# A decoder layer with 32 experts: the first norm's factor and shift moved behind the gather, routing reordered, the last expert weights in halves

## The chip, the cores and the metric

The kernel runs on one core of one Trainium2 chip. The metric is the device time of one execution in microseconds (us). The kernel before takes 873.96 us, the median of three runs (873.03, 873.96 and 874.01).

## What is computed

One layer of a decoder on 512 tokens of width 1024, in float32. A projection feeds a pooling mixer and a stick-breaking attention; their gated sum is projected out. Then come the first norm, a mixture of 32 experts in 4 groups, a gated embedding, and the second norm:

```
x = LayerNorm(alpha * x + merged @ w_o)                 (y * g + b, with ln1_g and ln1_b)
x = LayerNorm(alpha * x + HMoE(x) + sigmoid(x @ w_pg) * (p[i] @ w_pp))
...
g_idx = jnp.argmax(group_probs, axis=-1)
...
top_vals, top_idx = lax.top_k(sel_logits, TOP_K_IN_GROUP)
top_w = jax.nn.softmax(top_vals, axis=-1) * g_prob[:, None]
...
        h = jax.nn.silu(xt @ w_eg[g, e]) * (xt @ w_eu[g, e])
        y = y + (h @ w_ed[g, e]) * combine[:, g, e, None]
```

Each token goes to the two best experts of its best group. The expert weights are the bulk of what is read: 32 experts of 6 MB.

## The kernel before, in words

**Tiles and stages.** Tokens are in four blocks of 128 (tb 0 to 3). Products in float32 that need accuracy are made from a high and a low part (`mm3`, lines 143 to 145). After attention, `out_proj` multiplies the merged rows by w_o; `residual` adds alpha times x and takes statistics, `moments` and `shift` make factor and shift of a row, and `normalise` (ScalarE, L767) applies them. `gain` (L770) multiplies by the row g1 and `offset` (L773) adds the row b1, on VectorE or GpSimd; `affine` is both. `keep_high` (ScalarE, L786) and `keep_low` (L789) keep the result, called x1, as a high and a low part of 128x1024 per block, with its columns in another order.

**Routing.** `turn` transposes a block on TensorE (copies L595 on ScalarE, differences L596 on VectorE); `route` makes logits from the turned rows, which are not yet multiplied by g: the router's weights carry g and b. `fold_logits` (L617) adds the parts up. `choose` (L634 to L653, VectorE, for two blocks) finds group and experts and ends in the mask msk. `place` (L659 to L663) counts positions on TensorE; `count_tokens` (L670 on) and `rank` (L686 on) order the experts by their number of tokens. `order` holds their numbers, and the loads of all but three experts take the number from it.

**Experts.** Experts run in 12 units of 2, 3 or 4 (KINDS "pm" "pp" "qqq" "pppp" "m"; p is two, m three, q four). A unit has 128 slots for tokens, and `gather` (L848) fills them: x1's parts are multiplied by a one-hot matrix G, and `keep_slots` (L865, ScalarE, and L867, VectorE) copies a bank of PSUM into xg. `inner` (L907) makes two products with the weights eg and eu, `outer` (L1115) one with ed. `pair` runs a unit j: inner, outer, the gathers for the next two units, and the scatter of the unit before (`scatter_steps`). In unit 0, `renew` (L899) adds x1's parts up again for all four blocks in acc, and ScalarE multiplies them by alpha (L1085).

**Loads.** The weights are 192 chunks of 1 MB (`elist`). The tuple FIRST names 18 that are loaded ahead, with the pool that each lies in ("s8" is a pool of 8 tiles of 8 KB per partition, "wraw", "whi", "wlo", "acc" and "more" are others). From then on a chunk is loaded when a tile comes free: `eload_past` after a product in `inner` or `outer`, in the order `sequence`. SyncE issues all loads (L536, the halves L541) in this order. The last two chunks of the last unit are loaded in column halves. In units 3 to 6 the embedding runs between the products (`embedding`), with `split_transpose` turning x1.

**End.** In the last unit `split_acc` splits the accumulators; then, per block, a sum is opened with a product of the identity and these parts (L1290), the last unit's scatter is added (L1293), and statistics and the second norm follow.

Inside `with tc.manual_schedule()` each engine's instructions run in the order in which the program writes them.

Of the kernel before, what the change touches and what calls it, by code (L numbers as in the profile page):

```python
# [37 lines left out]
def layer_kernel(ctx: ExitStack, tc: tile.TileContext, x, p, w_in, w_pool, pool_scale, w_pu, w_au,  # L38
# [730 lines left out]
    def gain(tb, h, eng):  # L769
        eng.tensor_mul(acc[tb][:, halves[h]], acc[tb][:, halves[h]], g1[:, halves[h]])  # L770

    def offset(tb, h, eng):
        eng.tensor_add(acc[tb][:, halves[h]], acc[tb][:, halves[h]], b1[:, halves[h]])  # L773

    def affine(tb, h, eng):
        gain(tb, h, eng)
        offset(tb, h, eng)

# [607 lines left out]
```

## Time and profile before

| what | value |
| --- | --- |
| median of three runs | 873.96 us |
| the profiled execution | 873.73 us |
| span in its trace | 871.9 us |
| TensorE busy | 805.8 us (92%) |
| VectorE busy | 412.3 us (47%) |
| ScalarE busy | 214.2 us (25%) |
| GpSimd busy | 191.4 us (22%) |
| DMA | 241.89 MB, 276 GB/s read and written over the span |

PE is TensorE's products, PEld its weight loads, DVE VectorE, ACT ScalarE, POOL GpSimd, SP SyncE; SPq is SyncE's issuing of transfers. The times in a row count from the start of the span. A row of a timeline can stand for several equal instructions in a row (x4). Brackets at a row's end give the idle time of the engine before it, and what released it. PEclk is the clock that TensorE was granted, 1.00 being 2.4 GHz and 0.50 being 1.2 GHz. Busy shares are means over stages with different limits.

### The profile page before, as it was taken

What the parts mean: (1) busy time and instruction counts of PE and PEld (TensorE: products, weight loads), DVE (VectorE), ACT (ScalarE), POOL (GpSimd) and SP (SyncE); (2) the same over time, 40 slices, a digit from 0 to 9 for tenths busy, and PEclk for the clock granted to TensorE, in tenths of its full rate; (3) what the DMA queues carried; (4) which work ended last, traced back from release to release, by engine and by line L of the source; (5) the groups of instructions that cost most, each with busy time, mean ns of one, the idle gap of its engine ahead of it and who ended that gap; (6) DMA issues with size and microseconds to landing.
All of it is one profiled execution on the core that took longest, in us unless ns stands there. A gap on an engine that the chain in (4) does not pass through costs nothing.

```text
span 871.9 us, 11544 instructions
## 1 busy us (share of the span) xinstructions
PE 805.8 (92%) x4454; PEld 511.5 (59%) x4454; DVE 412.3 (47%) x691; ACT 214.2 (25%) x443; POOL 191.4 (22%) x176
## 2 busy tenths in 40 slices
PE   8999899899999998699999887899799999999983
PEld 7886677677768887635345333566375744545432
DVE  5278647645448858847442432221123244343437
ACT  3123444444461114313101011210220101100214
POOL 3333324224221235600000220231313000000225
PEclk9999999999999999689999989999999999999997
DMA  7431131222213786657999999999999999999992
GB/s 253 140 99 52 48 97 49 63 82 63 83 48 143 247 310 248 266 214 271 407 419 419 416 406 418 414 413 407 418 407 404 404 419 419 419 418 421 412 360 99
DMA packets 65787, 241.89 MB, mean 277 GB/s; under 512 B 12096, under 2 KB 32576, under 8 KB 41408
## 3 DMA queue, kind: packets, MB, share of 16 engines
q1 hardware_dynamic: 65728, 241.10, 71.1%
q8 instruction: 37, 0.61, 0.3%
q14 instruction: 22, 0.18, 0.1%
HBM read 238.99 MB, written 2.10 MB: 276 GB/s over the span
## 4 chain that ended last, share of the span: by engine, by line
PE 50%; DMA 11%; DVE 4%; POOL 2%; issue 1%; ACT 1%; SPq 1%; POOLq 0%; ACTq 0%; DVEq 0%
PE mm L907 18%; PE mm L1115 8%; PE xg_ps L848 6%; DMA ew<-in_w_eu_dram 4%; PE sc_ps L1148 4%; PE mm L143 3%; PE mm L145 3%; PE mm L144 3%; DMA ew<-in_w_ed_dram 3%; DMA pr<-in_p_dram 2%; DMA ew<-in_w_eg_dram 2%; PE pg_ps L144 1%; PE pg_ps L143 1%; PE pg_ps L145 1%; DVE acc L899 1%
## 5 line engine op out<-in xcount | busy, mean ns | idle before, releaser
L907 PE MATMUL mm<-ew,xg 128*32 128x512 f32 (+1 forms) x1088 | 189.5, 621 | 16.8 <-DMA ew<-in_w_eu_dram 11.1
L907 PEld LDWEIGHTS mm<-ew,xg 128*32 128x32 f32 (+1 forms) x1088 | 54.8, 125 | 137.3 <-issue 108.3
L1115 PE MATMUL mm<-ew,hT 128*32 128x512 f32 (+1 forms) x544 | 91.6, 597 | 3.0 <-DMA ew<-in_w_ed_dram 2.1
L132 POOL TENSOR_TENSOR wlo<-wraw,whi 128x1024 fp32r<-128x1024 f32 x23 | 69.1, 3003 | 108.4 <-DVE whi L127 52.5
L143 PE MATMUL mm<-xth,whi 128*128 128x512 f32 x224 | 91.6, 409 | 0.0
L145 PE MATMUL mm<-xth,wlo 128*128 128x512 f32 x224 | 88.6, 396 | 0.0
L144 PE MATMUL mm<-xtl,whi 128*128 128x512 f32 x224 | 88.3, 394 | 0.0
L1053 DVE TENSOR_TENSOR h<-mm,h 128x512 f32<-128x512 f32 x24 | 16.6, 692 | 128.9 <-PE mm L907 71.3
L848 PEld LDWEIGHTS xg_ps<-G,x 128*128 128x128 f32 x448 | 56.0, 198 | 13.6 <-issue 9.0
L848 PE MATMUL xg_ps<-G,x 128*128 128x256 f32 (+1 forms) x448 | 59.0, 290 | 1.2 <-DVE xg L867 1.2
L1149 DVE TENSOR_TENSOR acc<-acc,sc_ps 128x512 f32<-128x512 f32 x88 | 54.7, 681 | 6.6 <-PE sc_ps L1148 6.0
L1115 PEld LDWEIGHTS mm<-ew,hT 128*32 128x32 f32 (+1 forms) x544 | 24.7, 120 | 54.5 <-issue 46.1
L143 PEld LDWEIGHTS mm<-xth,whi 128*128 128x128 f32 x224 | 42.8, 191 | 9.5 <-issue 0.9
L144 PEld LDWEIGHTS mm<-xtl,whi 128*128 128x128 f32 x224 | 43.0, 192 | 8.8 <-issue 0.5
L145 PEld LDWEIGHTS mm<-xth,wlo 128*128 128x128 f32 x224 | 42.7, 190 | 9.3
L127 DVE CAST whi<-wraw 128x2048 fp32r<-128x2048 f32 x22 | 26.9, 1225 | 33.8 <-PE mm L144 16.6
L132 DVE TENSOR_TENSOR wlo<-wraw,whi 128x1024 fp32r<-128x1024 f32 x23 | 40.7, 1770 | 1.0
L1164 POOL TENSOR_TENSOR xf<-x 128x1024 f32<-128x1024 f32 x4 | 9.4, 2376 | 144.5 <-PE mm L907 144.5
L1137 POOL TENSOR_TENSOR accl<-acc,acch 128x512 fp32r<-128x512 f32 x8 | 10.5, 1337 | 137.7 <-ACT acch L1136 137.7
L1148 PE MATMUL sc_ps<-yh,Gt 128*128 128x512 f32 x88 | 37.8, 429 | 1.1 <-DVE sg L1220 1.1
L1220 DVE TENSOR_TENSOR sg<-pg_ps,sg 128x256 f32<-128x256 f32 x16 | 6.8, 425 | 65.4 <-ACT sg L1219 65.4
L144 PE MATMUL pg_ps<-pgl,xT 128*128 128x256 f32 x128 | 36.3, 284 | 0.7 <-POOL pgl L1200 0.7
(270 smaller groups left out, 1355.4 us busy)
## 6 DMA issues: line engine op xcount, KB each, us to landing
ew<-in_w_eg_dram SPq DMA_DIRECT2D x64, 1024.0 KB, 16.6
ew<-in_w_eu_dram SPq DMA_DIRECT2D x64, 1024.0 KB, 14.1
ew<-in_w_ed_dram SPq DMA_DIRECT2D x62, 1024.0 KB, 14.1
wraw<-in_w_in_dram SPq DMA_DIRECT2D x15, 1024.0 KB, 5.6
wraw<-in_w_o_dram SPq DMA_DIRECT2D x4, 1024.0 KB, 5.0
pgr<-in_w_pg_dram SPq DMA_DIRECT2D x4, 1024.0 KB, 17.3
wraw<-in_w_pu_dram SPq DMA_DIRECT2D x2, 1024.0 KB, 5.0
wraw<-in_w_au_dram SPq DMA_DIRECT2D x2, 1024.0 KB, 5.0
```

The costliest lines, as they stand in the source:

```text
L127: nc.vector.tensor_copy(hi, wraw[i])
L132: eng.tensor_sub(lo[:, j], wraw[i][:, j], hi[:, j].bitcast(F32))
L143: nc.tensor.matmul(o, lh, rh, start=start, stop=False)
L144: nc.tensor.matmul(o, lh, rl, start=False, stop=False)
L145: nc.tensor.matmul(o, ll, rh, start=False, stop=stop)
L848: nc.tensor.matmul(o[:, kx * 256:kx * 256 + n], x1[tb][:, i, cs], G[tb // 2][:, tb % 2].rearrange("p u s -> p (u s)"), start=whole and tb ...
L907: nc.tensor.matmul(o[cs], xgs[j][:, k, cs], ew[chunk0[j] + ne * (2 * n + k // 4) + i][:, k % 4], start=k == 0, stop=k == KD - 1)
L1053: nc.vector.tensor_mul(ht, o, ht)
L1115: nc.tensor.matmul(o[cs], hT[:, f, cs], ew[chunk0[j] + ne * (4 + f // 2) + i][:, f % 2, halves[c]], start=f == 0, stop=f == 3)
L1137: nc.gpsimd.tensor_sub(l, acc[tb][:, halves[c]], h.bitcast(F32))
L1148: nc.tensor.matmul(o, Gt[:, tb * 128:(tb + 1) * 128], y[c][i], start=i == 0, stop=i == 1)
L1149: nc.vector.tensor_add(acc[tb][:, cs], acc[tb][:, cs], o)
```

## The change

Factor and shift of the first norm. x1 is kept without them. As per-partition columns gq and bq, they are applied where gathered columns are copied out of PSUM (`keep_slots`: per bank two ScalarE and two VectorE instructions, of 128x128 each) and where x1 is turned for the embedding (`turn_x1`). The rows g and b lie together in one tile gb1 of the pool "s8", and `renew` applies them, two more VectorE instructions of 128x1024 for each block. Blocks 0 and 1 are renewed in the middle of unit 0, block 2 at its end, block 3 in unit 1; at the end of unit 1 the tile goes back to the loads. FIRST has 17 chunks instead of 18: chunk 27 is gone from it, and other chunks have other tiles.

Routing. `gain`, `offset` and `affine` go; of the eight low parts VectorE makes four (one before); folding the logits of block 1 comes earlier; `place(0)` stands before `turn(2)`; and two of the four gathers of blocks 0 and 1 come after `place(2)`.

End. All six ed chunks of the last unit come in column halves, the second halves last; the sums of blocks 0 and 1 are opened between the products of the second half. (A branch for too many tokens on an expert is changed too; it does not run with these inputs.)

```diff
-    g1 = lnt.tile([128, D], F32, name="g1")
-    b1 = lnt.tile([128, D], F32, name="b1")
-    nc.sync.dma_start(g1, rows_bcast(ln1_g, D))
-    nc.sync.dma_start(b1, rows_bcast(ln1_b, D))
+    gb1 = s8([128, 2, D], F32, "gb1")
+    gq, bq = (slp.tile([128, KD], F32, name=n) for n in ("gq", "bq"))
+    for i, (w, t) in enumerate(((ln1_g, gq), (ln1_b, bq))):
+        nc.sync.dma_start(gb1[:, i], rows_bcast(w, D))
+        nc.sync.dma_start(t, w[0].rearrange("(p k) -> p k", p=128))
...
-    FIRST = [(0, "s8"), (1, "s8"), (2, "s8"), (4, "s8"), (5, "wraw"), (6, "whi"), (8, "wlo"), (9, "wraw"), (10, "s8"),
-             (11, "s8"), (12, "s8"), (15, "s8"), (18, "whi"), (21, "wlo"), (3, "acc"), (24, "more"), (27, "more"),
-             (7, "acc")]
+    FIRST = [(0, "s8"), (1, "s8"), (2, "s8"), (4, "wraw"), (5, "whi"), (6, "wlo"), (8, "wraw"), (9, "s8"), (10, "s8"),
+             (11, "s8"), (12, "s8"), (15, "whi"), (18, "wlo"), (3, "acc"), (21, "more"), (24, "more"), (7, "acc")]
...
-        if i < len(elist) - 2:
+        tail = range(len(elist) - 2 * n_experts[-1], len(elist))
+        if i not in tail:
             nc.sync.dma_start(ew[i], source(i))
-        elif i == len(elist) - 1:
-
-            for c in range(2):
-                for j in (i - 1, i):
-                    nc.sync.dma_start(ew[j][:, :, halves[c]], source(j)[:, :, halves[c]])
+            return
+
+        for c, js in ((0, (i,)), (1, tail if i == tail[-1] else ())):
+            for j in js:
+                nc.sync.dma_start(ew[j][:, :, halves[c]], source(j)[:, :, halves[c]])
...
     def keep_slots(us, o, kb):
         o = o.rearrange("p (k e s) -> p k e s", k=2, e=2)
-        ks = slice(2 * kb, 2 * kb + 2)
-        nc.scalar.activation(xgs[us[0]][:, ks], o[:, :, 0], AF.Copy)
-        if len(us) > 1:
-            nc.vector.tensor_copy(xgs[us[1]][:, ks], o[:, :, 1])
+        for i in range(2):
+            k = 2 * kb + i
+            nc.scalar.activation(xgs[us[0]][:, k], o[:, i, 0], AF.Identity, scale=gq[:, k:k + 1], bias=bq[:, k:k + 1])
+            if len(us) > 1:
+                nc.vector.tensor_scalar(xgs[us[1]][:, k], o[:, i, 1], gq[:, k:k + 1], bq[:, k:k + 1], op0=OP.mult,
+                                        op1=OP.add)
...
-    def renew(b):
-
-        new_acc(b)
-        for tb in (b, b + 1):
-            hi, lo = (x1[tb][:, i].rearrange("p (k m) -> p m k", k=KD).bitcast(F32) for i in range(2))
-            nc.vector.tensor_add(acc[tb].rearrange("p (m k) -> p m k", k=KD), hi, lo)
+    def renew(tb):
+
+        if tb % 2 == 0:
+            new_acc(tb)
+        hi, lo = (x1[tb][:, i].rearrange("p (k m) -> p m k", k=KD).bitcast(F32) for i in range(2))
+        nc.vector.tensor_add(acc[tb].rearrange("p (m k) -> p m k", k=KD), hi, lo)
+        nc.vector.tensor_mul(acc[tb], acc[tb], gb1[:, 0])
+        nc.vector.tensor_add(acc[tb], acc[tb], gb1[:, 1])
+        nc.scalar.activation(acc[tb], acc[tb], AF.Copy, scale=ALPHA)
...
-        gain(0, 0, dve)
         shift(1)
-        offset(0, 0, dve)
-        affine(0, 1, pool)
...
-        keep_low(0, 0, pool)
-        keep_low(0, 1, pool)
...
         residual(2, 1, o)
         moments(2)
-        gain(1, 0, dve)
+        keep_low(0, 0, pool)
+        keep_low(0, 1, dve)
         shift(2)
-        offset(1, 0, dve)
-        affine(1, 1, pool)
...
-        out_proj(3, 1, o, parts, range(2, 4))
+        out_proj(3, 1, o, parts, range(2, 3))
         fold_logits(lg2, 1)
         choose(lg2, 0)
...
         moments(3)
-        turn(2, lambda: shift(3))
-        keep_low(1, 1, pool)
-        eload_first(15)
-        affine(2, 1, pool)
+        place(0)
+        turn(2)
+        keep_high(1, (0,))
+        shift(3)
         normalise(3)
-        place(0)
-        one_hots(G[0], (0,), 0)
-        gain(2, 0, dve)
...
         route(2)
+        keep_high(1, (1,))
+        keep_low(1, 0, pool)
+        keep_low(1, 1, dve)
+        one_hots(G[0], (0,), 0)
         turn(3)
-        offset(2, 0, dve)
-        affine(3, 0, dve)
-        affine(3, 1, pool)
+        keep_high(2)
+        keep_low(2, 0, pool)
         route(3)
...
-        for kb in range(3):
+        for kb in range(2):
             gather(G, xs[kb], kb, (0, 1))
-        keep_high(2)
         keep_high(3)
+        keep_low(2, 1, dve)
         choose(lg2, 2)
-        keep_low(2, 0, pool)
-        keep_low(2, 1, pool)
-        keep_low(3, 1, pool)
-        keep_low(3, 0, dve)
-        eload_first(18)
+        keep_low(3, 0, pool)
         place(2)
-        gather(G, xs[3], 3, (0, 1))
+        keep_low(3, 1, dve)
+        eload_first(17)
+        for kb in range(2, 4):
+            gather(G, xs[kb], kb, (0, 1))
...
                 for f in range(4):
+                    if c and f in (0, 2):
+                        open_sum(f // 2)
                     outer(j, hT, f, c, o[c])
...
-        return Gt, [weighted(o[c], ws) for c in range(2)]
+        y = [weighted(o[c], ws) for c in range(2)]
+        if j == 0:
+            renew(2)
+        elif j == 1:
+            free.append("s8")
+            eload_past(done[0])
+        return Gt, y
```

VectorE's instructions from the positions of blocks 0 and 1 (posm) to the start of the second choosing (lg), before; g_2339 and b_2340 are the rows g and b, x1T a turned block:

```order
L663 SCALAR_TENSOR_TENSOR posm<-pos_ps,msk 128x64
L836 TENSOR_TENSOR G<-iota_c,posm 128x256
L770 TENSOR_TENSOR acc<-acc,g_2339 128x512
L596 TENSOR_TENSOR x1T<-x1T_ps,x1T 128x512 x2
L773 TENSOR_TENSOR acc<-acc,b_2340 128x512
L770 TENSOR_TENSOR acc<-acc,g_2339 128x512
L773 TENSOR_TENSOR acc<-acc,b_2340 128x512
L634 TENSOR_TENSOR lg<-lg_ps,lbias 128x80
```

The same stretch of VectorE now; x_2802 and x_2853 are the kept x1 of blocks 1 and 2:

```order
L666 SCALAR_TENSOR_TENSOR posm<-pos_ps,msk 128x64
L599 TENSOR_TENSOR x1T<-x1T_ps,x1T 128x512 x2
L765 TENSOR_SCALAR rs<-mv,rs 128x1
L783 TENSOR_TENSOR x_2802<-acc,x_2802 128x64x8
L830 TENSOR_TENSOR G<-iota_c,posm 128x256
L599 TENSOR_TENSOR x1T<-x1T_ps,x1T 128x512 x2
L783 TENSOR_TENSOR x_2853<-acc,x_2853 128x64x8
L637 TENSOR_TENSOR lg<-lg_ps,lbias 128x80
```

Four multiplications and additions by the rows are gone from this piece; two low parts (L783, before L789) and the turn of block 2 have come in.

TensorE's instructions from the positions of blocks 2 and 3 (pos_ps) to the counts (ct_ps), before; xg_ps_2826 is the last of four banks of gathered slots, x1_2688 and x1_2742 are blocks 0 and 1:

```order
L659 MATMUL pos_ps_2952<-msk_2358,strict_67 128x64
L661 MATMUL pos_ps_2952<-msk_2358,ones_66 128x64 x2
L662 MATMUL pos_ps_2952<-msk_2358,ones_66 128x32
L848 MATMUL xg_ps_2826<-G_2544,x1_2688 128x128 x2
L848 MATMUL xg_ps_2826<-G_2544,x1_2742 128x128 x2
...
L670 MATMUL ct_ps_2968<-msk_2358,ones_66 128x32 x4
```

The same now, with the banks xg_ps_2809 and xg_ps_2810; the two rows of a bank come twice, before as now:

```order
L662 MATMUL pos_ps_2926<-msk_2361,strict_67 128x64
L664 MATMUL pos_ps_2926<-msk_2361,ones_66 128x64 x2
L665 MATMUL pos_ps_2926<-msk_2361,ones_66 128x32
L842 MATMUL xg_ps_2809<-G_2545,x1_2685 128x128 x2
L842 MATMUL xg_ps_2809<-G_2545,x1_2802 128x128 x2
...
L842 MATMUL xg_ps_2810<-G_2545,x1_2685 128x128 x2
L842 MATMUL xg_ps_2810<-G_2545,x1_2802 128x128 x2
...
L673 MATMUL ct_ps_2953<-msk_2361,ones_66 128x32 x4
```

Eight gather products (one bank) have moved from ahead of the positions to behind them.

TensorE's end now, from the last turn of one-hots (gt_ps) on; the first 16 products are those of the first column half. Before, all 32 stood in one row, `L1115 MATMUL mm<-ew,hT 32x512 x32`, and the sums behind it:

```order
L883 MATMUL gt_ps<-ident,outs 128x128 x4
L1113 MATMUL mm<-ew,hT 32x512 x16
L1145 MATMUL sum_ps<-acch,one 128x512
L1145 MATMUL sum_ps<-accl,one 128x512
...
L1113 MATMUL mm<-ew,hT 32x512 x8
...
L1113 MATMUL mm<-ew,hT 32x512 x8
L1312 MATMUL sum_ps<-yh,Gt 128x512
```

Two blocks' opening sums (four L1145 rows each, before L1290 behind the products) have moved in: the first ahead of the second half's products, the second in their middle.

## Rows read from the trace of the kernel before

**Rows 1.** Windows: us, each engine's busy time (instructions), TensorE's clock, DMA share, GB/s.

```profile
360.00:376.60 16.60, 12.72 (x50) 9.73 (x50) 8.02 (x35) 2.22 (x4) 2.27 (x2) 0.50 0.28 100
412.00:414.00 2.00, 2.00 (x24) 0.65 (x20) 0.00 (x0) 0.00 (x0) 0.00 (x0) 1.00 0.00 0
416.00:838.00 422.00, 395.93 (x2512) 208.94 (x2505) 138.45 (x236) 56.33 (x100) 49.82 (x32) 0.98 1.01 415
840.00:844.00 4.00, 3.39 (x22) 0.57 (x18) 0.52 (x1) 1.34 (x3) 4.00 (x4) 1.00 1.03 383
```

**Rows 2.** Timeline of SyncE's queue: start, duration (us), engine, line, operation.

```profile
379.01 8.39 SPq L536 DMA_DIRECT2D ew<-in_w_eg_dram  x4
...
414.63 3.43 SPq L536 DMA_DIRECT2D ew<-in_w_eg_dram  x4
...
827.82 9.09 SPq L541 DMA_DIRECT2D ew<-in_w_ed_dram  x4
```

**Rows 3.** Timeline of VectorE during the routing.

```profile
338.27 2.01 DVE L770 TENSOR_TENSOR acc<-acc,g 128x512 f32<-128x512 f32 x1
...
342.43 0.23 DVE L634 TENSOR_TENSOR lg<-lg_ps,lbias 128x80 f32<-128x80 f32 x1
...
343.92 1.47 DVE L642 SCALAR_TENSOR_TENSOR sel<-pen,lg 128x64 f32<-128x64 f32 x1
...
346.70 0.22 DVE L653 TENSOR_TENSOR msk<-oh 128x64 fp32r<-128x64 f32 x1
...
363.50 0.22 DVE L653 TENSOR_TENSOR msk<-oh 128x64 fp32r<-128x64 f32 x1
```

**Rows 4.** Timeline of TensorE from the first gathers to the counts.

```profile
355.28 2.87 PE L848 MATMUL xg_ps<-G,x 128*128 128x128 f32 x24
363.88 0.39 PE L659 MATMUL pos_ps<-msk,strict 128*128 128x64 f32 x1 [5.72 <-DVE msk L653]
...
364.72 1.95 PE L848 MATMUL xg_ps<-G,x 128*128 128x128 f32 x8
366.47 0.97 PE L670 MATMUL ct_ps<-msk,ones 128*128 128x32 f32 x4
```

**Rows 5.** Groups by line and form, 334 to 366: | busy us, mean ns | idle before.

```profile
L789 POOL TENSOR_TENSOR x<-acc,x 128x512 fp32r<-128x512 f32 x7 | 11.5, 1660 | 3.0 <-ACT x L786 2.8
L786 ACT ACTIVATE x<-acc 128x512 fp32r<-128x512 f32 x8 | 8.5, 1144 | 2.4 <-DVE acc L773 2.3
...
L596 DVE TENSOR_TENSOR x1T<-x1T_ps,x1T 128x512 fp32r<-128x512 f32 x6 | 4.0, 684 | 1.6 <-ACT x1T L595 1.6
...
L595 ACT ACTIVATE x1T<-x1T_ps 128x512 fp32r<-128x512 f32 x6 | 3.4, 596 | 1.8 <-PE x1T_ps L592 1.8
...
L767 ACT ACTIVATE acc<-acc,rs 128x512 f32<-128x512 f32 x4 | 3.0, 808 | 5.7 <-DVE rs L762 5.7
...
L613 ACT ACTIVATE lt<-lg_ps 72x128 f32<-72x128 f32 x3 | 0.8, 273 | 2.8 <-PE lg_ps L611 2.8
...
L789 DVE TENSOR_TENSOR x<-acc,x 128x512 fp32r<-128x512 f32 x1 | 1.0, 1035 | 0.0
```

**Rows 6.** Groups of VectorE by line and form, 378 to 416.

```profile
L899 DVE TENSOR_TENSOR acc<-x 128x1024 f32<-128x1024 f32 x4 | 9.7, 2480 | 0.0
...
L881 DVE TENSOR_TENSOR Gw<-Gw,comb 128x512 f32<-128x512 f32 x1 | 0.7, 691 | 0.0
```

**Rows 7.** Timeline of TensorE in unit 0.

```profile
405.50 4.03 PE L848 MATMUL xg_ps<-G,x 128*128 128x256 f32 x32 [1.23 <-DVE xg L867]
```

**Rows 8.** Issues, 836 to 850: operation xcount, KB each, median us from issue to landing.

```profile
ew<-in_w_ed_dram SPq DMA_DIRECT2D x2, 512.0 KB, 9.6
```

**Rows 9.** Timeline of TensorE, the last products.

```profile
843.82 5.34 PE L1115 MATMUL mm<-ew,hT 128*32 128x512 f32 x42 [0.32 <-DMA ew<-in_w_ed_dram]
```

**Rows 10.** Timeline of VectorE, statistics of the second block.

```profile
852.69 1.29 DVE L1230 BATCH_NORM_STATS2 st<-sum_ps 128x6 f32<-128x512 f32 x2 [0.19 <-PE sum_ps L1293]
```

**Rows 11.** Timeline of GpSimd, a low part of block 1.

```profile
343.75 1.56 POOL L789 TENSOR_TENSOR x<-acc,x 128x512 fp32r<-128x512 f32 x1
```

More of the change, by code (lines that the diff above doesn't have):

```diff
@@ L725, in relabel @@
         full = [128, 2, NT, E]
-        t, u = (lnt.tile(full, F32, name=n, tag=t) for n, t in (("by_rank", "g1"), ("by_slot", "b1")))
+        t, u = (lnt.tile(full, F32, name=n) for n in ("by_rank", "by_slot"))
         r2, s2 = (lnt.tile([128, 2, NT, 1], F32, name=n) for n in ("r2", "s2"))
@@ L767, in normalise, with keep_high @@
             nc.scalar.activation(acc[tb][:, cs], acc[tb][:, cs], AF.Identity, scale=rs[:, :1], bias=rs[:, 1:])
[L769 to L777, printed above, removed]
     def turned(t, h):
         return t.rearrange("p (k m) -> p m k", k=KD)[:, 64 * h:64 * h + 64]
-    def keep_high(tb):
-        x1[tb] = res.tile([128, 2, D], F32R, name="x1", bufs=4)
-        for h in range(2):
+    def keep_high(tb, hs=(0, 1)):
+        if 0 in hs:
+            x1[tb] = res.tile([128, 2, D], F32R, name="x1", bufs=4)
+        for h in hs:
             nc.scalar.activation(turned(x1[tb][:, 0], h), acc[tb][:, halves[h]].rearrange("p (m k) -> p m k", k=KD), AF.Copy)
@@ L793, in layer_kernel @@
     parts = [wnext() for _ in range(2)]
-    eload_first(4)
+    eload_first(3)
     for kk in range(2):
@@ L819, in layer_kernel @@
     parts = [wnext() for _ in range(2)]
-    eload_first(8)
+    eload_first(7)
     xgs = {}
@@ L953, in layer_kernel @@
         normalise(2)
-        keep_high(1)
-        out_proj(3, 1, o, parts, range(2, 4))
+        out_proj(3, 1, o, parts, range(2, 3))
         fold_logits(lg2, 1)
         choose(lg2, 0)
-        keep_low(1, 0, pool)
-        out_proj(3, 1, o, parts, range(4, 8))
-        eload_first(14)
+        out_proj(3, 1, o, parts, range(3, 8))
+        eload_first(13)
         residual(3, 1, o)
         moments(3)
-        turn(2, lambda: shift(3))
-        keep_low(1, 1, pool)
-        eload_first(15)
-        affine(2, 1, pool)
+        place(0)
+        turn(2)
+        keep_high(1, (0,))
+        shift(3)
         normalise(3)
-        place(0)
-        one_hots(G[0], (0,), 0)
-        gain(2, 0, dve)
         xs = [mm("xg_ps") for _ in range(4)]
@@ L1055, in pair @@
                 embed(1)
+                if j == 1:
+                    renew(3)
             if four:
@@ L1081, in pair @@
         if j == 0:
-            for b in (0, 2):
-                renew(b)
-                for tb in (b, b + 1):
-                    nc.scalar.activation(acc[tb], acc[tb], AF.Copy, scale=ALPHA)
+            renew(0)
+            renew(1)
         embed(3)
@@ L1138, in split_acc, with open_sum @@
             acc2[tb, c] = h, l
-    acc2, outs = {}, []
+    acc2, outs, total = {}, [], []
+    def open_sum(tb):
+        total.append([bank("sum_ps") for bank in ((zz, zz), (tt, tt), (mm, mm), (mm, mm))[tb]])
+        for c in range(2):
+            for i in range(2):
+                nc.tensor.matmul(total[tb][c], acc2["one"], acc2[tb, c][i], start=i == 0, stop=False)
     def scatter_steps(Gt, y):
@@ L1165, in rows, with turn_x1 @@
             return [xf[:, i] for i in range(2)]
+        def turn_x1(xt, src):
+            for h in range(2):
+                pt = tt("x1T_ps")
+                t = ex.tile([128, 4, 128], F32, name="x1t", tag="pph", bufs=1)
+                for i in range(4):
+                    k = 4 * h + i
+                    nc.tensor.transpose(pt[:, i * 128:(i + 1) * 128], src[:, k * 128:(k + 1) * 128], ident)
+                for i in range(4):
+                    k = 4 * h + i
+                    nc.vector.tensor_scalar(t[:, i], pt[:, i * 128:(i + 1) * 128], gq[:, k:k + 1], bq[:, k:k + 1],
+                                            op0=OP.mult, op1=OP.add)
+                hi, lo = (xt[:, i, 4 * h:4 * h + 4] for i in range(2))
+                nc.scalar.activation(hi, t, AF.Copy)
+                nc.vector.tensor_sub(lo, t, hi.bitcast(F32))
         assert kept[0] >= 2
@@ L1285, in layer_kernel @@
         for tb in range(NT):
-            total.append([bank("sum_ps") for bank in ((zz, zz), (tt, tt), (mm, mm), (mm, mm))[tb]])
-            for c in range(2):
-                for i in range(2):
-                    nc.tensor.matmul(total[tb][c], acc2["one"], acc2[tb, c][i], start=i == 0, stop=False)
+            if tb > 1:
+                open_sum(tb)
             for c in range(2):
@@ L1318, in layer_kernel @@
                         nc.tensor.transpose(pt[:, k * 128:(k + 1) * 128], t[:, kx * 128:(kx + 1) * 128], ident)
-                    nc.vector.tensor_copy(x1T2[:, 4 * h:4 * h + 4, tb * 128:(tb + 1) * 128],
-                                          pt.rearrange("p (k t) -> p k t", k=4))
+                    for k in range(4 * h, 4 * h + 4):
+                        nc.vector.tensor_scalar(x1T2[:, k, tb * 128:(tb + 1) * 128], pt[:, k % 4 * 128:(k % 4 + 1) * 128],
+                                                gq[:, k:k + 1], bq[:, k:k + 1], op0=OP.mult, op1=OP.add)
             wov = ov.tile([128, NT, E], F32, name="wov")
```

11 lines of the change are left out of this document (5 added, 6 removed).

## The prediction

> **What bounds the kernel now.** I read the windows first [rows 1]. From 416 to 838 us the 16 DMA engines are full (share 1.01, 415 GB/s), so in that stretch work on the other engines is worth nothing; before it, from 412 to 414, they stand still. The end of the kernel is therefore: the moment at which the stream starts for good, plus the bytes still to come over 415 GB/s, plus the tail. SyncE's timeline gives that moment [rows 2]. Every load of an expert chunk after the prefetched ones waits for a slot that TensorE's products give back; the first starts at 379.01, and the one that ends the dry stretch starts at 414.63, in unit 1. The change counts by what it does to the time of 414.63, to the bytes that are left then, and to the tail.
>
> Backwards from 414.63 stands TensorE in unit 0, and ahead of it the routing. There VectorE's timeline [rows 3] and TensorE's [rows 4] are read together: VectorE runs without a gap into the masks of blocks 2 and 3, which end at 363.72, and TensorE waits 5.72 us for them. Its clock is then 0.50, the 1.2 GHz level, from 360 to 376.6 [rows 1], and what is queued there (positions, gathers, counts, ranks, the first products) is serial.
>
> **The change, part by part.** The sum is made against the profiled execution, 873.73 us, 0.23 below the median of 873.96.
>
> A, the masks of blocks 2 and 3. VectorE's list before them loses six multiplications and additions by g and b (1.65 to 2.01 us each, the first of them in [rows 3]) and gains three low parts. I lay the new list end to end from 338.35, where the first gain now starts:
> - low part of block 0, 1.04 as the one row of VectorE alone [rows 5], and a small shift: choosing of blocks 0 and 1 can start at 339.8 instead of 342.43;
> - it took 4.49 (342.43 to 346.92), of which one small instruction was 1.47 [rows 3], a stall; with part of that gone I take 4.1, to 343.9;
> - residual and statistics of block 3, two of 128x512 at .684 [rows 5] and small ones, 1.85, to 345.75; position mask, two differences of turned blocks at .684 and a shift, to 347.6;
> - now ScalarE decides: two normalisations at .808, the other half of block 1's high part and the copy of the logits, 1.14 and .27, two copies for the turn of block 3 at .596, two high parts of block 2 at 1.14 [rows 5], and another .27, with small waits for TensorE, to 354.0;
> - the last low part of block 2, 1.04 alone, 1.66 as GpSimd's beside others [rows 5], to 355.2, and choosing 4.3, to 359.5.
> That is **4.2 us earlier**. Bounds: 1.7, if every low part takes as long as the gain that it replaces and choosing as long as now; 6.5, if neither choosing stalls and ScalarE's waits vanish.
>
> B, eight gather products that ran inside TensorE's wait now run after the second positions, ahead of the counts: 8 took 1.75 (364.72 to 366.47 [rows 4]), so **+1.75**; at the full clock 24 took 2.87, and it would be .96. The first new load should thus start 2.45 earlier.
>
> C, unit 0. TensorE there waits 1.23 for slots to be emptied at 405.50 [rows 7], behind the accumulators' renewal (four additions of 2.48, one ending just before [rows 6]). Now two blocks are renewed at that place, with a multiplication and an addition of 128x1024 each; each of these is two of the .69 that 128x512 takes [rows 6], so 2 x (2.48 + 4 x .69) = 10.5 for 9.7, +.8. Emptying a bank takes four alternating instructions instead of two; ScalarE's with factor and shift takes .81 per 512, a plain one .60 [rows 5], +.2. Together **+1.0** (0.3 if most hides under the products, 1.4 if all of it shows). Block 2's renewal stands at the end of unit 0, and block 3's in unit 1, some 5 us each, where VectorE is idle before the next product of h; if that cover failed, scattering into block 2 would be late, in a stretch that DMA bounds.
>
> D, one chunk fewer. The s8 slot that holds the two rows keeps out the chunk 27, and comes back only at the end of unit 1. The dry stretch shows that all loads with slots are done by 414.63, so one chunk of 1,048,576 bytes more is left: at 415 GB/s **+2.5**.
>
> E, the end. Before, after 843.82 TensorE has 42 product rows in 5.34 us without a wait [rows 9], since the first columns' products come late too. The last half was issued by 836.91 [rows 2] and lands 9.6 later [rows 8], 846.5. Now all six last chunks come in column halves; 4.2 MB more move at 383 GB/s, as 840 to 844 shows, in place of 415 [rows 1], +.85: 847.35. Left then are 10 product rows, 1.27, so 848.6 against 849.16, −.55. The sum opened early saves the .19 that VectorE waits for the second block [rows 10], −.15: **−.7** (−1.6 if halves run at 415 and the products keep up; +.6 if they come no sooner than now). By the Trainium skill, "DMA: Bandwidth & Descriptors", Specifications, a transfer of 512 bytes or more already runs at line rate, so pieces of 2 KB would cost nothing and E would be .85 lower; the trace's 383 speaks against it, and I keep the trace's.
>
> F, gq and bq, the later stages. Their loads stand with the rows', ahead of the routing; turning x1 in the embedding adds four small VectorE instructions per bank, within 416 to 838, where VectorE is busy 138 of 422 us [rows 1]. 0. If DMA were not full there, this would count.
>
> Sum: −4.2 + 1.75 + 1.0 + 2.5 − .7 = +.35, so **874.1 us**; its own range is 872.0 (A 1.2 better, E at its lower bound) to 876.6 (A 1.2 worse, E at its upper bound). What a measurement of this kernel can tell from no change is 0.2%, 1.75 us.
>
> **Rivals.**
> R1, the clock stays up. The half clock stands after TensorE's wait of 5.72 [rows 4]. If earlier masks leave it busy enough to stay at 2.4 GHz, half of the 12.7 us of TensorE work in 360 to 376.6 and half of B go: 7.2 less, 866.9. Against it: some wait remains, since eight products fewer fill it. Chance .12.
>
> R2, slower: VectorE's low parts wait for GpSimd's. Low parts now run on both at once in three blocks. The place that decides is the last low part of block 2 and choosing after it, with GpSimd's low parts beside. For it: the gain at 338.27 took 2.01 while GpSimd worked, and VectorE's one low part 1.04; the small instruction of 1.47 ended at 345.39, just when a low part on GpSimd did, 345.31 [rows 3, 5, 11]. Then A is its lower bound 1.7, and the time 876.6. It decides from masks later than about 360.9 on: A is then 2.8, and the sum over 1.75. Chance .24. The Trainium skill, "SBUF — State Buffer", Terms, has it that VectorE and GpSimd share a port pair that is locked for a whole instruction, so that "the loser fully blocks"; by that rule it would be this rival.
>
> R3, faster: the routing gives its upper bound of 6.5, because GpSimd too loses its multiplications and additions by g and b, and so neither choosing stalls. Then the sum is −1.95, 871.8. Chance .20.
>
> R4, the missing slot costs nothing, so D is 0 and the time 871.6: only if the stream after 414.63 has room to make up a chunk. The share of 1.01 over 422 us speaks against it. Chance .04.
>
> **How the numbers follow.** The forecast keeps .40. The larger part of its own range lies within 0.2%. Faster: R1, R3, R4, .36; same .40; slower .24. The range goes from 868.0 (R3 with E at its lower bound and R4 beside them, 868.4, rounded down) to 877.0 (R2 with C's upper bound); what it leaves out is R1 and a little on the upper side, under .2.
>
> **What would show it.** In the profile after: the second mask at about 359.5; the first load after the prefetched ones at about 376.5; the clock 0.5 from the wait to the first products; the load after the dry stretch at about 413.2, with no DMA before it for longer than now; DMA full from there on; second halves at some 385 GB/s; the last products .5 us closer to the last landing. It is wrong if the clock is at 1.0 from 360 to 376, if the mask comes after 361 or before 358, or if the DMA share falls below 1 between the dry stretch and 838.

## The result, and the profile after

The changed kernel takes 880.37 us (median of four runs, 879.65 to 881.43) against 873.99 for the kernel before in the same session (873.03 to 874.46): ratio 1.0080 [1.0062, 1.0099], slower. Forecast were 874.1, with a range of 868.0 to 877.0. The profiled execution took 879.65; its span is 877.8, 5.9 longer than before.

Five marks, each a row on SyncE or TensorE, cut the span into pieces that can be compared (us from the span's start; behind each, the difference to before and the term of the prediction that it answers to):

| mark | before | after | the piece grew by | term |
| --- | --- | --- | --- | --- |
| first load behind the prefetched ones | 379.01 | 376.96 | −2.05 | A and B: −2.45 |
| unit 1's first products | 409.46 | 408.78 | +1.37 | C: +1.0 |
| eight eg loads of units 4 and 5, ahead of the embedding | 464.76 | 466.33 | +2.25 | D: +2.5 |
| last six eu loads | 798.48 | 804.15 | +4.10 | F: 0 |
| end of the span | 871.9 | 877.8 | +0.23 | E: −0.7 |

The timeline of SyncE's queue, after (start, duration, line), which answers to [rows 2]:

```profile
376.96 8.39 SPq L539 DMA_DIRECT2D ew<-in_w_eg_dram  x4
...
415.88 3.77 SPq L539 DMA_DIRECT2D ew<-in_w_eg_dram  x4
...
466.33 17.77 SPq L539 DMA_DIRECT2D ew<-in_w_eg_dram  x8
...
804.15 22.88 SPq L539 DMA_DIRECT2D ew<-in_w_eu_dram  x6
```

The same queue before, the two rows that were not shown:

```profile
464.76 17.79 SPq L536 DMA_DIRECT2D ew<-in_w_eg_dram  x8
...
798.48 22.88 SPq L536 DMA_DIRECT2D ew<-in_w_eu_dram  x6
```

Most of the loss lies between the last two rows, 333.72 us before and 337.82 after: in the stretch that [rows 1] shows as full of DMA, and where the prediction priced everything at nothing. The windows after:

```profile
360.00:376.60 16.60, 16.60 (x60) 10.88 (x60) 3.56 (x20) 2.42 (x6) 0.00 (x0) 0.50 0.28 102
...
416.00:838.00 422.00, 390.34 (x2482) 207.32 (x2478) 160.01 (x286) 69.41 (x122) 49.82 (x32) 0.97 1.01 411
...
550.00:600.00 50.00, 45.08 (x329) 27.41 (x330) 13.35 (x26) 10.91 (x17) 14.53 (x8) 0.93 0.95 376
...
840.00:844.00 4.00, 3.75 (x22) 2.51 (x24) 3.39 (x6) 0.89 (x2) 0.00 (x0) 1.00 1.04 383
```

And one window before:

```profile
550.00:600.00 50.00, 45.96 (x347) 29.59 (x336) 11.74 (x20) 9.55 (x15) 14.53 (x8) 1.00 1.02 412
```

Over 422 us the DMA share still reads 1.01; what fell is the rate, 415 to 411 GB/s, and that is 4 us (422 x 4/415). One short window shows where: from 550 to 600 us the share is .95 and the rate 376. It lies at the end of unit 4, where the banks for the next units are emptied and the embedding uses the same engines. TensorE's timeline there, before:

```profile
544.65 1.03 PE L592 MATMUL x1T_ps<-ident,xf 128*128 128x128 f32 x8
546.66 0.66 PE L887 MATMUL gt_ps<-ident,Gw 128*128 128x128 f32 x4 [0.98 <-DVE xT L596]
547.25 3.64 PE L1115 MATMUL mm<-ew,hT 128*32 128x512 f32 x32
...
554.75 1.06 PE L907 MATMUL mm<-ew,xg 128*32 128x512 f32 x6
557.19 3.62 PE L907 MATMUL mm<-ew,xg 128*32 128x512 f32 x26 [1.38 <-DMA ew<-in_w_eg_dram]
...
561.78 0.39 PE L144 MATMUL pg_ps<-pgl,xT 128*128 128x256 f32 x1 [0.65 <-POOL pgl L1200]
```

After, with one row of unit 0 ahead of them (it answers to [rows 7]) and the last products behind (they answer to [rows 9]):

```profile
404.78 4.07 PE L842 MATMUL xg_ps<-G,x 128*128 128x256 f32 x32 [2.46 <-DVE xg L862]
...
546.55 1.03 PE L1180 MATMUL x1T_ps<-ident,xf 128*128 128x128 f32 x8
549.92 0.66 PE L883 MATMUL gt_ps<-ident,Gw 128*128 128x128 f32 x4 [2.33 <-DVE x1t L1183]
550.50 5.34 PE L1113 MATMUL mm<-ew,hT 128*32 128x512 f32 x32
...
559.80 3.64 PE L906 MATMUL mm<-ew,xg 128*32 128x512 f32 x32
...
567.80 0.39 PE L144 MATMUL pg_ps<-pgl,xT 128*128 128x256 f32 x1 [4.04 <-POOL pgl L1222]
...
852.07 1.06 PE L1113 MATMUL mm<-ew,hT 128*32 128x512 f32 x6
853.39 1.90 PE L1113 MATMUL mm<-ew,hT 128*32 128x512 f32 x10 [0.25 <-DMA ew<-in_w_ed_dram]
```

TensorE waits 1.35 longer for VectorE at the turn of one-hots; the 32 outer products behind that wait take 5.34 instead of 3.64, at a granted clock of .57 in 551 to 555; and it waits 3.39 longer for pgl, the low part of the embedding's weight. Before, the stretch had a reserve: TensorE waited 1.38 us for weights (554.75 to 557.19), DMA being the later one, and the 32 products around that wait, in two rows of 1.06 and 3.62, took 1.04 longer than the single row of 3.64 now. 1.35 + 1.70 + 3.39 − 1.38 − 1.04 is 4.02. The starts of the rows say the same: from the turn of x1 (x8) to the first product with pgl 17.13 us pass before and 21.25 after, +4.12, and the stage lost 4.10. Weights' slots come free from these products, and SyncE can load no sooner.

Why pgl is late is in the timelines of ScalarE and GpSimd, after:

```profile
557.99 0.46 ACT L860 ACTIVATE xg<-xg_ps,bq,gq 128x128 f32<-128x128 f32 x1 [4.59 <-PE xg_ps L842]
...
560.85 0.46 ACT L860 ACTIVATE xg<-xg_ps,bq,gq 128x128 f32<-128x128 f32 x1 [0.48 <-DVE xg L862]
561.20 1.90 ACT L1221 ACTIVATE pgh<-pgr 128x2048 fp32r<-128x2048 f32 x1
```

```profile
563.24 4.51 POOL L1222 TENSOR_TENSOR pgl<-pgr,pgh 128x2048 fp32r<-128x2048 f32 x1 [48.72 <-DMA ew<-in_w_eg_dram]
```

ScalarE empties two banks from 557.99 to 561.2, taking turns with VectorE; the high part pgh is queued behind that, and GpSimd's pgl starts .14 after pgh ends, as it does before, so pgh is what it waits for, whatever releaser the row names. Before, pgh ran at 555.13, .38 behind the start of the next unit's products (554.75); now it runs 1.40 behind it (559.80). So the suspicion is the emptying in `keep_slots`, for which the prediction had one sum of +.2 in unit 0.

### The profile page after: what moved, and what is told of

Same layout as the page of the kernel before. It is cut to its first block, busy times and chain, and to the rows that moved or that the text cites. A ratio compares the mean times of both kernels' runs of the same rounds, so it can differ in the third digit from the quotient of the medians.

```text
span 877.8 us, 11647 instructions
## 1 busy us (share of the span) xinstructions
PE 809.3 (92%) x4454; PEld 513.4 (58%) x4454; DVE 429.1 (49%) x746; ACT 228.5 (26%) x471; POOL 174.8 (20%) x165
## 4 chain that ended last, share of the span: by engine, by line
PE 28%; DMA 19%; DVE 2%; issue 2%; POOL 1%; SPq 1%; ACT 1%; POOLq 0%; DVEq 0%; ACTq 0%
PE mm L906 10%; DMA ew<-in_w_eu_dram 7%; PE mm L1113 6%; DMA ew<-in_w_ed_dram 5%; DMA ew<-in_w_eg_dram 5%; PE xg_ps L842 3%; PE sc_ps L1154 3%; DMA pr<-in_p_dram 2%; PE pg_ps L143 1%; PE pg_ps L144 1%; PE pg_ps L145 1%; SPq L539 1%; POOL pgl L1222 1%; PE hT_ps L1058 0%; PE gt_ps L883 0%
## 5 line engine op out<-in xcount | busy, mean ns | idle before, releaser
L906 PE MATMUL mm<-ew,xg 128*32 128x512 f32 (+1 forms) x1088 | 186.0, 615 | 14.2 <-DMA ew<-in_w_eu_dram 9.9
L842 PEld LDWEIGHTS xg_ps<-G,x 128*128 128x128 f32 x448 | 59.6, 207 | 15.6 <-issue 12.3
L842 PE MATMUL xg_ps<-G,x 128*128 128x256 f32 (+1 forms) x448 | 62.6, 300 | 2.5 <-DVE xg L862 2.5
L860 ACT ACTIVATE xg<-xg_ps,bq,gq 128x128 f32<-128x128 f32 x56 | 24.7, 456 | 89.2 <-PE xg_ps L842 79.6
```

The costliest lines, as they stand in the source:

```text
L842: nc.tensor.matmul(o[:, kx * 256:kx * 256 + n], x1[tb][:, i, cs], G[tb // 2][:, tb % 2].rearrange("p u s -> p (u s)"), start=whole and tb ...
L860: nc.scalar.activation(xgs[us[0]][:, k], o[:, i, 0], AF.Identity, scale=gq[:, k:k + 1], bias=bq[:, k:k + 1])
L906: nc.tensor.matmul(o[cs], xgs[j][:, k, cs], ew[chunk0[j] + ne * (2 * n + k // 4) + i][:, k % 4], start=k == 0, stop=k == KD - 1)
```

## The experiments

Three theories for the loss. T1: `turn_x1` puts more small VectorE instructions in front of what TensorE waits for. T2: the embedding's p comes too late; TensorE waits 8.5 us for it after the change. T3: emptying a gathered bank in four instructions with factor and shift instead of two plain copies. "Stage" below is the time from the eight eg loads to the last six eu loads (before 333.72, after 337.82), "unit 0" the time from the first new load to unit 1's first products (before 30.45, after 31.82). Ratios are to the kernel before on the same chip.

**e1, the change with x1 turned without factor and shift.**

```diff
-            turn_x1(xt, xf[tb])
+            split_transpose(xt, xf[tb])
```

> The changed kernel with x1 turned for the embedding as before, without factor and shift (this part of the computation is left out). Theory T1 (the serial chain of four VectorE instructions, a copy and a difference in one buffer per half block makes the turned one-hots wait and the clock fall behind that wait): TensorE's wait ahead of them goes from 2.3 back to about 1.0 us, the half clock behind it and part of the later wait for GpSimd go, and of the 4.1 us that the stream of weights loses between 465 and 720 us some 2.5 come back: about 877.5. Theory T2 (the rows p land one chunk later in the stream): no change, 880.4. Theory T3 (slower emptying of the gathered banks holds up the split of w_pg): no change beyond 0.5.

Measured: 876.97 us, 1.0051 [1.0039, 1.0063]; stage 337.94, as long as after the change, and TensorE still waits 4.0 for pgl. T1 does not explain the stage. The median is .3% below the change's all the same; e6 and e7 come back to that.

**e2 and e4, p two chunks earlier in the change, and two chunks later in the kernel before.**

```diff
-    EMB = {3: (0, 0, 0, 1, 0, 0), 4: (1, 1, 1, 1, 1, 1), 5: (2, 2, 1, 2, 2, 1), 6: (2, 2, 1, 2, 1, 1)}
+    EMB = {3: (0, 0, 1, 0, 0, 0), 4: (1, 1, 1, 1, 1, 1), 5: (2, 2, 1, 2, 2, 1), 6: (2, 2, 1, 2, 1, 1)}
```

(In e4 the 1 stands in the fifth place.)

> The changed kernel with the first step of the embedding (the load of p) one place earlier in unit 3, so that it stands two chunks earlier in the stream of loads than in the change and one earlier than before. T2: TensorE's wait for p falls from 8.5 to about 3.5 us, the DMA engines no longer run dry between 555 and 600 us, and about 4 of the 6.4 us come back: 876.4. T1 and T3: the wait for p was free, since DMA was full then; the time stays at 880.4 and the dry stretch stays.

> The kernel before with the load of p one place later in unit 3, two chunks later in the stream. T2: TensorE waits about 5 us longer for p, 10 in all, and DMA runs dry later, so 2 to 4 us are lost, 876 to 878. T1 and T3: the wait is covered by the full DMA, 874.

Measured: e2 879.31 us, 1.0080 [1.0067, 1.0093], stage 338.25, although the wait for p fell from 8.5 to 3.6. e4 873.44, 1.0003 [0.9993, 1.0014], stage 333.92, although TensorE now waited 9.9 for p. T2 falls from both sides: a wait of 9.9 us on the busiest engine cost nothing at that place.

**e3, the change without the rows' tile and the renewal's multiplication and addition.**

```diff
-    gb1 = s8([128, 2, D], F32, "gb1")
...
-        nc.vector.tensor_mul(acc[tb], acc[tb], gb1[:, 0])
-        nc.vector.tensor_add(acc[tb], acc[tb], gb1[:, 1])
```

(FIRST is then the tuple of before, with 18 chunks.)

> The changed kernel without the tile of the rows g and b: 18 chunks ahead as before, in the tiles as before, and blocks renewed without factor and shift (this part of the computation is left out). The missing chunk D should give back 2.2 to 2.5 us, and the shorter renewal in unit 0 some 0.8; p then stands in the stream where it stood before. T2: the dry stretch in the embedding goes too, together about 873.5. T1 or T3 alone: the dry stretch stays, about 877.5.

Measured: 873.45 us, 1.0010 [0.9996, 1.0024]. The dry piece is 55.09, as before (55.30), so the 2.25 there belongs to the missing slot. Unit 0 is 29.31. The stage is still 336.34, 2.6 too long; 1.48 of it came back, since the outer products kept the full clock behind the same wait as after the change:

```profile
544.78 0.66 PE L882 MATMUL gt_ps<-ident,Gw 128*128 128x128 f32 x4 [2.33 <-DVE x1t L1177]
545.37 3.64 PE L1107 MATMUL mm<-ew,hT 128*32 128x512 f32 x32
```

So the median meets T2's figure by a sum of other parts: slot, unit 0 and clock.

**e5, the change with the plain copies of before.**

```diff
-        for i in range(2):
-            k = 2 * kb + i
-            nc.scalar.activation(xgs[us[0]][:, k], o[:, i, 0], AF.Identity, scale=gq[:, k:k + 1], bias=bq[:, k:k + 1])
...
+        ks = slice(2 * kb, 2 * kb + 2)
+        nc.scalar.activation(xgs[us[0]][:, ks], o[:, :, 0], AF.Copy)
+        if len(us) > 1:
+            nc.vector.tensor_copy(xgs[us[1]][:, ks], o[:, :, 1])
```

> The changed kernel with gathered banks emptied as before, one copy per engine without factor and shift (this part of the computation is left out). T3: a pair of banks is emptied about 2 us sooner, TensorE's wait ahead of the turned one-hots falls from 2.3 to about 1, the wait for GpSimd's pgl from 4.0 to about 2, and the stream loses about 2 us instead of 4.1 between 465 and 800; with 0.5 to 1 us more in unit 0: about 877.3 against 880.4 of the change (beside a kernel before of 874.0). T4 (with the new FIRST two slots are kept back for the embedding one step earlier in unit 4, so that loads stand still): the loss of 4 stays, about 879.8.

Measured: 871.58 us, 0.9991 [0.9976, 1.0007]; stage 333.19, unit 0 30.66. The whole loss of the stage is gone, more than the 2 us that T3 had been given, and T4 of the expectation falls.

**e6 and e7, e3 and e5 together, and with e1's edit as well.**

> The run without the tile of rows (18 chunks ahead, tiles as before; renewal without factor and shift left out), with banks emptied by plain copies too (left out as well). T3: of the 2.6 us that that run still lost between 465 and 800 some 2 come back, and half a us in unit 0: 2.5 us faster than it, about 0.2% faster than before. T1 (turning x1 for the embedding is what is left): not more than 0.7 us faster than it.

> The same with x1 turned without factor and shift too, so that only the new order of the routing, shorter renewal and the halves at the end are left of the change. What T1 costs shows as the difference to the run ahead: T1 about 1.5 us, T3 nothing. The stream should lose nothing between 465 and 800; the time should be 3 to 5 us under before.

Measured: e6 867.58 us, 0.9948 [0.9932, 0.9963]; e7 867.63, 0.9952 [0.9935, 0.9969]; stages 333.77 and 333.24. Where banks are emptied quickly, the turn with factor and shift costs nothing. The .3% of e1 against the change appears only under slow emptying and is not in the profile's marks; its cause stays open. Against e5, the rows and their slot cost .43%.

**e14, the kernel before with the change's emptying alone,** its factor ones and its shift zeros.

```diff
+    gq = cst.tile([128, KD], F32, name="gq")
+    nc.vector.memset(gq, 1.0)
+    bq = cst.tile([128, KD], F32, name="bq")
+    nc.vector.memset(bq, 0.0)
...
-        ks = slice(2 * kb, 2 * kb + 2)
-        nc.scalar.activation(xgs[us[0]][:, ks], o[:, :, 0], AF.Copy)
...
+        for i in range(2):
+            k = 2 * kb + i
+            nc.scalar.activation(xgs[us[0]][:, k], o[:, i, 0], AF.Identity, scale=gq[:, k:k + 1], bias=bq[:, k:k + 1])
...
```

> The kernel before with its banks emptied exactly as in the change, by four instructions of 128 elements with a factor and a shift per partition, which are one and zero here: 0.46 and 0.41 us each in place of 0.38 and 0.42 for twice the elements, 3.5 us per pair of banks in place of 1.6. If the slow emptying alone makes the loss (T3): the stream loses 2.5 to 4.5 us between 465 and 800, ratio 1.003 to 1.006. If it takes x1's turning beside it: no more than 1.0015.

Measured: 878.86 us, 1.0080 [1.0065, 1.0095]: as slow as the whole change, from this one edit; unit 0 32.86, stage 337.62. That the totals are equal is chance: the stage gives 3.90, and unit 0 2.41, more than in the change, because its gathers ran at the half clock (5.53 us for 4.03 before); that puts the ratio above the 1.006 expected. In the stage, SyncE's queue, the window and TensorE's rows of e14 resemble those of the change, with the pgl wait the same to the digit:

```profile
464.73 17.77 SPq L540 DMA_DIRECT2D ew<-in_w_eg_dram  x8
...
802.35 22.87 SPq L540 DMA_DIRECT2D ew<-in_w_eu_dram  x6
```

```profile
550.00:600.00 50.00, 45.38 (x339) 29.17 (x332) 12.31 (x22) 10.36 (x16) 14.50 (x8) 0.95 0.97 383
```

```profile
547.34 0.66 PE L893 MATMUL gt_ps<-ident,Gw 128*128 128x128 f32 x4 [1.83 <-DVE xT L600]
547.93 5.34 PE L1121 MATMUL mm<-ew,hT 128*32 128x512 f32 x32
...
565.13 0.57 PE L148 MATMUL pg_ps<-pgl,xT 128*128 128x256 f32 x1 [4.04 <-POOL pgl L1206]
```

T3 is shown as the cause of the stage's loss: without the slow emptying the loss is gone (e5), with it alone it comes (e14).

**e10 and v1, two other ways to empty.** e10 is the kernel before with four plain copies of 128x128 per bank. v1 is the change with both units' slots in one tile, so that one instruction per engine takes a column of both units, with factor and shift:

```diff
+        t = slp.tile([128, 2, KD, 128], F32, name="xg", bufs=1)
...
+        nc.scalar.activation(x[:, k], o[:, 0], AF.Identity, scale=gq[:, k:k + 1], bias=bq[:, k:k + 1])
+        k += 1
+        nc.vector.tensor_scalar(x[:, k], o[:, 1], gq[:, k:k + 1], bq[:, k:k + 1], op0=OP.mult, op1=OP.add)
```

> The kernel before with its banks emptied by four copies of 128 elements per bank in place of two of 256, nothing else: T3's cost alone. T3: the units in which the embedding turns x1 and splits w_pg lose 3 to 5 us, as in the change (TensorE's wait for pgl about 4 us in place of 0.7): ratio 1.004 to 1.006. If emptying costs only together with the rest of the change: no more than 1.001.

> The changed kernel, whole in what it computes, with the slots of two units in one tile, so that a bank is emptied by two instructions of 256 elements (ScalarE one, VectorE the other) in place of four of 128. If the number of serial instructions per bank is the cost (T3), nearly all of what the plain copies gave back comes back here, though factor and shift are still applied: 872 to 874, a ratio of 0.999 to 1.002 to before, and the stream loses less than 1 us between 465 and 800. If reading factor and shift itself is the cost (T5), little comes back: 879.

Measured: e10 873.85 us, 1.0008 [0.9998, 1.0018], stage 333.92; v1 872.70, 0.9994 [0.9981, 1.0006], stage 333.32. Groups by line and form, 380 to 720 (out<-in xcount | busy, mean ns | idle before), first before, then after, v1 and e10:

```profile
L867 DVE COPY xg<-xg_ps 128x256 f32<-128x256 f32 x16 | 6.7, 424 | 38.9 <-ACT xg L865 38.9
L865 ACT ACTIVATE xg<-xg_ps 128x256 f32<-128x256 f32 x17 | 6.4, 382 | 52.6 <-PE xg_ps L848 52.6
```

```profile
L860 ACT ACTIVATE xg<-xg_ps,bq,gq 128x128 f32<-128x128 f32 x32 | 14.5, 458 | 40.2 <-PE xg_ps L842 32.6 <-DVE xg L862 7.7
...
L862 DVE TENSOR_SCALAR xg<-xg_ps,gq,bq 128x128 f32<-128x128 f32 x32 | 13.1, 410 | 33.1 <-ACT xg L860 33.1
```

```profile
L864 ACT ACTIVATE xg<-xg_ps,bq,gq 128x256 f32<-128x256 f32 x16 | 8.9, 563 | 39.1 <-PE xg_ps L842 39.1
L866 DVE TENSOR_SCALAR xg<-xg_ps,gq,bq 128x256 f32<-128x256 f32 x16 | 8.6, 544 | 31.6 <-ACT xg L864 31.6
```

```profile
L868 DVE COPY xg<-xg_ps 128x128 f32<-128x128 f32 x32 | 9.2, 291 | 37.8 <-ACT xg L866 37.8
L866 ACT ACTIVATE xg<-xg_ps 128x128 f32<-128x128 f32 x32 | 8.8, 277 | 49.6 <-PE xg_ps L848 43.8 <-DVE xg L868 5.8
```

VectorE's idle time in all four is ended by ScalarE, and ScalarE's in part by VectorE where a bank takes four instructions: the two take turns at one bank. Added up, two banks, as a unit's end has them, take 2 x (.382 + .424) = 1.6 us before, 2.3 in e10, 2.2 in v1 and 4 x (.458 + .410) = 3.5 after. Not all of it stands in the way, since the first bank is emptied while TensorE fills the second: pgh starts .38 behind the next unit's first product before, .58 in v1, .92 in e10 and 1.40 after. In v1 the same place reads:

```profile
545.36 0.66 PE L886 MATMUL gt_ps<-ident,Gw 128*128 128x128 f32 x4 [1.64 <-DVE x1t L1186]
545.94 3.64 PE L1116 MATMUL mm<-ew,hT 128*32 128x512 f32 x32
...
560.73 0.38 PE L144 MATMUL pg_ps<-pgl,xT 128*128 128x256 f32 x1 [1.66 <-POOL pgl L1225]
```

The runs side by side (us; "path" is the time from the turn of x1 to the first product with pgl):

| run | emptying, two banks | 32 outer products | path | stage |
| --- | --- | --- | --- | --- |
| before | 1.6 | 3.64 | 17.13 | 333.72 |
| e5 | 1.6 | 3.64 | 17.58 | 333.19 |
| e10 | 2.3 | 3.64 | 18.01 | 333.92 |
| v1 | 2.2 | 3.64 | 18.05 | 333.32 |
| e3 | 3.5 | 3.64 | 19.55 | 336.34 |
| e14 | 3.5 | 5.34 | 20.65 | 337.62 |
| after | 3.5 | 5.34 | 21.25 | 337.82 |

A path up to .9 longer than before costs the stage .2 or less, as a reserve there would have it; a longer one costs 2.6 to 4.1. So 1.3 us less emptying can return the whole 4 us. The half clock makes 1.70 of the path in e14 and after; why e3 was spared it was not found. Neither four plain instructions (e10, for which T3 had forecast 3 to 5 us) nor factor and shift in two (v1, where T5 had forecast 879) cost the stage anything; both together do.

**e8, the kernel before with the change's end alone** (six chunks in halves, two sums opened between the products).

> The kernel before with the end of the change alone: six chunks in column halves, second halves last, and two sums opened between the products. The prediction's E says 0.7 us faster; the trace of the change, whose last product came 0.4 us later behind the stream, says no change or 0.2 us slower.

Measured: 872.96 us, 1.0005 [0.9993, 1.0016]; from the last six eu loads to the end 74.01, against 73.42. No gain.

**e11 and e12, the kernel before with 17 chunks ahead and one s8 tile held.** In e11 the tile had no later use, so its slot came free at once (the first load came at 372.74, right behind the ranking): 872.72 us, 0.9995 [0.9986, 1.0003], which says nothing on D. e12 mends that with a read at unit 1's end:

```diff
+    hold = s8([128, 2, D], F32, "hold")
...
+        if j == 1:
+            nc.vector.tensor_copy(mhalf2, hold[:, 0, :1])
+            free.append("s8")
+            eload_past(done[0])
```

> The kernel before with 17 chunks ahead, the tiles of the change, and a slot of the pool held back without use until the end of unit 1: the prediction's D alone. D says one chunk at the stream's rate: 2.5 us, ratio 1.0029; if the stream makes it up (R4), 1.000.

> The kernel before with 17 chunks ahead and the slot really held (it is read once more at the end of unit 1, so the first load behind the ranking waits for TensorE again): the prediction's D alone. D: from the start of unit 1 to the load at 464 us 57.6 us pass in place of 55.3, and the kernel takes 2.5 us more, ratio 1.0029. If the stream makes up a chunk (R4): 55.3 and 1.000.

Measured: e12 874.70 us, 1.0025 [1.0015, 1.0036]; the piece from unit 1's first products to the eg loads is 57.65 against 55.30, +2.35, and nothing later makes it up (stage 333.82).

**v4 and e13, better than both.** v4 is v1 with block 1's renewal moved from the middle of unit 0 to behind the turn of one-hots, where VectorE has less to do, and its multiplication by alpha to the unit's end; e13 is v4 with three of the four gathers of blocks 0 and 1 again ahead of choosing.

```diff
-            renew(1)
...
+                if j == 0:
+                    renew(1)
```

> The same with the renewal of block 1 in unit 0 moved behind the first emptying of banks, so that TensorE no longer waits 2.5 us for it there. If that wait is on the path, unit 1 starts 1 to 2 us sooner and the kernel is that much faster than the run ahead: 871 to 872.5, at or below the kernel before.

> The repaired version (slots in one tile, renewal spread) with three of the four gathers of blocks 0 and 1 ahead of the second choosing, as in the kernel before: the prediction's B undone. B: counts and first products 1.8 us sooner at the half clock, so 1.8 us faster than the repaired version, 0.9955 to before. If VectorE's mask, not TensorE, sets the positions and the eight products then delay these by as much: no change, 0.9975.

Measured: v4 870.26 us, 0.9975 [0.9961, 0.9988], unit 0 29.31; e13 870.50, 0.9965 [0.9951, 0.9980]. Both beat the kernel before and the change; between them the intervals decide nothing. In e13, 3.60 us lie between second mask and counts, in v4 4.44: .84 back, not B's 1.75, because the gathers then run at the half clock (24 in 5.36) and end behind the mask.

## Why the prediction was wrong

**F is the step that failed,** and with it the premise that work on the other engines is worth nothing from 416 to 838. "0. If DMA were not full there, this would count" covered the turn of x1 and the rest of the later stages; the emptying of banks had been priced in C, in unit 0 alone. But it recurs at every pair of units, and at the end of unit 4 DMA stayed full only because TensorE had 1.38 us in hand. A mean share of 1.01 over 422 us could not show that; a row in the stretch, TensorE's wait for weights, did. Measured: +4.10 where 0 stood, and the emptying alone makes 3.90 in the same stage (e14). The sign named for this, a DMA share below 1 between the dry stretch and 838, is what came (.95 in 550 to 600), and the mean over the whole stretch hides it after the change too.

**C** had the size nearly right and the parts wrong: +1.37 for +1.0. With plain copies (e5) unit 0 is .21 longer than before, so most of the rest is the emptying priced at .2: the wait at the gathers is 2.46 instead of 1.23 [rows 7]. It shows there only where VectorE comes late from the renewal: without the rows, which shortens that, unit 0 is 29.31 with the slow emptying (e3) and 29.32 with the plain copies (e6). The .2 came from one row with factor and shift and one plain, both of 512 elements (.81 and .60), at which the fixed part of an instruction does not show. By the Trainium skill, "ScalarE: Activation LUTs", What ACT_TABLE_LOAD costs, an instruction takes 186 ns + .833 ns per element and some 93 ns for each per-partition operand; estimates from it are 293, 399, 479 and 585 ns for the four forms, and the rows say 277, 382, 458 and 563. The trace agrees within 6%, and by that rule ScalarE's part of a bank, two of 479 for one of 399, would have been seen to more than double.

**A and B** came out at −2.05 for −2.45 by luck, from two errors that nearly cancel. The second mask stands 5.8 earlier (363.50 to 357.69, predicted 4.2, bound 6.5), and so before 358, which the prediction had named as a sign of being wrong. VectorE's timeline after:

```profile
338.60 1.08 DVE L783 TENSOR_TENSOR x<-acc,x 128x512 fp32r<-128x512 f32 x1
...
340.26 0.23 DVE L637 TENSOR_TENSOR lg<-lg_ps,lbias 128x80 f32<-128x80 f32 x1
...
352.48 1.74 DVE L783 TENSOR_TENSOR x<-acc,x 128x512 fp32r<-128x512 f32 x1 [0.22 <-ACT x L780]
354.04 0.24 DVE L637 TENSOR_TENSOR lg<-lg_ps,lbias 128x80 f32<-128x80 f32 x1
...
357.69 0.22 DVE L656 TENSOR_TENSOR msk<-oh 128x64 fp32r<-128x64 f32 x1
```

The second choosing starts at 354.04, forecast 355.2, and takes 3.87 for 4.3. The prediction has ScalarE's list last from 347.6 to 354.0, although its own terms add up to 6.8 and so to 354.4; ScalarE went through it from 346.99 to 352.44. Low parts alone take 1.05 to 1.08, for the 1.04 taken; the one at 352.48 takes 1.74, .70 more, and GpSimd's low part ran beside it for .68. A small instruction (a cast) of either choosing takes .52 and .97 and ends within .03 of the end of a low part on GpSimd. So the waiting that R2 feared exists, in three places, and did not bring R2's late mask. But from mask to first load it is now 19.05 instead of 15.29, +3.76. Of this 1.71 is B as priced: 16 gathers behind the positions take 3.46, where eight took 1.75. The rest is the clock, which is .50 until about 376.6 as before: the last eight products ahead of the load now take 3.68 at the half clock, for 1.94, and eight gathers 1.97, for 1.65. R1 did not come in this profile. In seven of the nine profiles with the change's routing the first load came at 373.0 to 374.8, in two near 377.0, this one among them; in six with the routing of before (without e11) it came at 376.7 to 379.1, so one profile's −2.05 can be off by some 2 us. What sets the moment at which the half clock ends was not found.

**D** was right: 2.25 here, 2.35 in e12, for 2.5. R4 falls.

**E** missed by .9: +.23 for −.7 (e8: nothing). The halves move at 383 GB/s as predicted, but the last ten products waited .25 for the last landing and took 1.90 instead of 1.27. The last product ends at 855.29 against 849.16, 6.1 later where the stream was 5.7 later: .45 back, not .55 forward. Behind it .23 were saved, for the .15 taken for the sums opened early. A single profile tells little here: from the last six eu loads to the end it is 72.7 to 74.9 in the runs with the change's end and 73.4 to 74.1 in the others. By its medians e8's interval, −.6 to +1.4 us, just leaves out the −.7.

R2, the slower rival, gave 876.6 for a late mask that did not come; the time beyond it came from a case that was no rival.

## What to carry to other kernels

Where a stream of transfers bounds a stage only because other engines keep just ahead of it, look for the smallest reserve in the stage, the shortest waits that end with the transfer, and price every repeated piece of work against that, not against the mean share. Work on PSUM banks that two engines empty in turn was a serial chain here: count its instructions at the small shape, with their operands, and see what stands behind it on both queues. Factor and shift on the way out of PSUM are cheap if instructions grow rather than multiply: v1 does the same arithmetic in half as many instructions and is as fast as the kernel before.
